# Latent attention: when the second half of the queries is made

## The chip, the cores and the metric

The kernel runs on one core of a Trainium2 chip. The metric is the device time of one launch in microseconds (us); the kernel before takes 2556.23 us (median of 3 runs, 2555.82 to 2557.56). All stages below run in that launch. Five engines work side by side and wait for each other through semaphores: TensorE (PE, matmuls into the PSUM banks), VectorE (DVE), ScalarE (ACT), GpSimd (POOL), and SyncE (SP), which starts the transfers of the weights. PEld is TensorE's loading of the stationary operand.

## The reference, cut to what matters

Two residual blocks work on 512 tokens of width 1024. The first has a mixer, a cross attention to a memory and a gated FFN; the second has two layers, of which the last holds the stage that is changed, `mla_mixer`, a latent attention of 8 heads:

```
lat = h @ w_in                                  # 768 query latent | 256 kv latent | 64 rotary key
q  = rmsnorm(cq, q_norm) @ w_q_up               # 8 heads x (128 plain + 64 rotary)
kv = rmsnorm(ckv, kv_norm) @ w_kv_up            # 8 heads x (128 key + 128 value)
q  = rope_tail(rmsnorm(q, q_head_norm)); k = rope_tail(rmsnorm(k, k_head_norm))
s  = q k^T * 192**-0.5, causal; p = softmax(s); o = p v
y  = o.reshape(S, 1024) @ w_out
```

All matrix products are kept near float32: each operand is split into a high part and a low part, and a product is made of three matmuls (high x high, low x high, high x low).

## The kernel before, in words

Everything is stored transposed, channels on the 128 partitions and the 512 tokens along the free axis. `linear` (L180 on) makes one output tile of 128 channels after another: a weight unit is fetched on SP's queue (`fetch`, L137), split by `cook` into `whi` on ACT (L146) and `wlo` on DVE (L148), and for each piece of the contraction `mm3` issues three matmuls (L176 to L178) into one PSUM bank. Then an eviction function reads the bank. There are three buffers each for the raw, the high and the low weights.

PSUM has eight banks, in groups with a tag each: `ps` 2, `sc` 2, `pt` 2, `po` 1, `mi` 1. SBUF tiles of 128 x 512 come from pools with tags too: `xs` 16, `cv` 9, `pr` 2, `m` 16, `q` 17, `t` 7. A tile of a tag can only be taken when one of that tag's buffers has been given back by its last reader.

The order of each engine's instructions is written by a planner while the program is built: it goes through the program text in a simulated time of its own and lets an engine take, of the instructions that are ready by its reckoning, the one that stands first in the text. On the chip every engine then runs its list strictly in that order.

The stage `mla` makes, in this order of the text: the kv and query latents; the raw keys of all heads (`kraw`); `values(0)`, the values of heads 0 to 3; then the queries, in twelve tiles of 128 channels (three for each pair of heads: two plain tiles and one that holds the rotary part of both). `ev_q` (L1083) evicts a query tile: it squares it (L320) and sums the squares with small matmuls into the bank `qsum` (L216), then splits a plain tile into `qn` (tag `xs`) or turns a rotary tile (`rope`, L459 to L464, on DVE and POOL) and packs it with `stack` (L472 on ACT, L474 on DVE) into `qp` (tag `cv`). After every sixth tile `inner_rstd` makes the scale of four heads, `fcol`: it reads `qsum` (L225), turns it on PE, and finds the inverse root in three Newton rounds of small DVE instructions (L235 to L243, ending at L271).

`key(h)` finishes a head's key: `spread` (two matmuls, L313 and L314) brings its scale across the partitions, ACT copies it to `bs` (L1104), POOL multiplies `kraw` (L1106) and the shared rotary key (`kp`, L1111) with it, and each is split into high (ACT, L193) and low (L195; on POOL for `kn`, on DVE for `kp`). `key(0)` is made after the sixth query tile, the other keys by `scores`.

`scores(h)` makes four blocks of 128 queries: three matmuls with the plain key, two with the rotary key (L1137 and L1138), one that adds the causal mask (L1140). `softmax_rows` takes the maximum (DVE, L445), multiplies it with the scale (L446), exponentiates (ACT, L448), inverts the sum (DVE, L449) and normalises (POOL, L450). `attend(h)` transposes the probabilities (L132, tag `pt`), splits them into `pth` and `ptl`, and multiplies them with the values into the bank `po`; the result is split into `os`. The order of the text is

```
scores(0); then for h = 0 to 7: scores(h + 1), attend(h), and values(1) after h == V_AT
```

with `V_AT` 1; `values(1)` are the values of heads 4 to 7. The product with `mla_w_out` and the last FFN follow.

Of the kernel before, what the change touches and what calls it, by code (L numbers as in the profile page):

```python
# [17 lines left out]
P = 128  # L18
# [43 lines left out]
class Kern:  # L62
# [939 lines left out]
                                scalar2=None, op0=ALU.mult)  # L1002


    V_AT = 1
    MLA_TAGS = ("pt", "mi")
    KEYS_EARLY = 1
    KEY_AT = 1
# [2 lines left out]
    def mla(self):  # L1011
        nc = self.nc
        a = self.a
        self.TR_TAG, self.BC_TAG = self.MLA_TAGS
        xs, R = self.pre("mixg1")
        rb = self.bcast(R)
        cq, ckv, st = [], [], {}
        sqs = {"q": [], "kv": []}
        cos, sin = self.cos2, self.sin2

        def ev_cq(nt, ps):
            sqs["q"] = self.gather(sqs["q"], self.square(ps), nt == 5)
            cq.append(self.split(ps, self.v("gql", nt), "q", name="cq"))

        def ev_ckv(nt, ps):
            sqs["kv"] = self.gather(sqs["kv"], self.square(ps), nt == 7)
            ckv.append(self.split(ps, self.v("gkvl", nt - 6), "q", name="ckv"))

        def ev_kpe(nt, ps):
            t = self.t("cv", name="kpe")  # L1030
            nc.vector.tensor_tensor(out=t, in0=ps, in1=rb, op=ALU.mult)
            st["sqpe"] = self.square(t)
            st["kpr"] = self.rope(t, "gkp", "gkps", cos, sin)

        w = a["mla_w_in"]
        tags = ("ps", "ps", "sc", "sc")
        ones = self.c("ones")
        self.linear(w, [6, 7], xs, ev_ckv, tags)
        self.linear(w, [8], xs, ev_kpe, ("sc",))
        Rkv = self.inner_rstd(self.sums([(ones, q) for q in sqs["kv"]]), 256, R)  # L1040
        bkv = self.bcast(Rkv, "pr")
        self.linear(w, range(6), xs, ev_cq, tags)
        Rq = self.inner_rstd(self.sums([(ones, q) for q in sqs["q"]]), 768, R)

        kraw = []
        pesum = self.y("pesum")[:, :8]
        nc.vector.tensor_copy(pesum.rearrange("p (j r) -> p j r", j=4), self.columns(
            self.sums([(self.c("blk64")[:, :32], st["sqpe"])]), 192, EPS, 2))
        ksum = self.ps("mi", "ksum")
        for u in range(2):  # L1050
            ws = self.tiles(self.load_unit(a["mla_w_k"][u]), 8)
            for hh in range(4):
                h = 4 * u + hh
                ps = self.ps(tags[hh])
                for k in range(2):
                    self.mm3(ps, ws[2 * hh + k], ckv[k], k == 0, k == 1)
                self.sums([(self.c("selh")[:, 32 * h:32 * h + 32], self.square(ps))], ps=ksum,
                          start=h == 0, stop=h == 7)
                t = self.t("m", name="kraw")
                nc.vector.scalar_tensor_tensor(out=t, in0=ps, scalar=self.v("gkn"), in1=bkv,  # L1060
                                               op0=ALU.mult, op1=ALU.mult)
                kraw.append(t)
        Rk = self.expand(self.key_rstd(ksum[:, :P], pesum, Rkv), 8, "pr")

        vs = [[None] * 4 for _ in range(2)]

        def values(c):
            hi, lo = self.load_unit(a["mla_w_v"][c])
            for tt in range(4):
                ts_ = slice(tt * P, (tt + 1) * P)  # L1070
                ps = self.ps(tags[tt])
                for k in range(2):
                    self.mm3(ps, (ckv[k][0][:, ts_], ckv[k][1][:, ts_]),
                             (hi[:, k * S:(k + 1) * S], lo[:, k * S:(k + 1) * S]), k == 0, k == 1)
                vs[c][tt] = self.split(ps, Rkv[:, tt:tt + 1],
                                       "m" if c == 0 or tt < 2 else "cv", name="v")

        values(0)

        qn, qp, fcol = [], [], []  # L1080
        qsum = self.ps("po", "qsum")

        def ev_q(nt, ps):  # L1083
            p, r = nt // 3, nt % 3
            sq = self.square(ps)
            i, o = p % 2, P * (p // 2)
            sel = self.c("selh")[:, 32 * (2 * i + r):32 * (2 * i + r) + 32] if r < 2 \
                else self.c("blk64")[:, 32 * i:32 * i + 32]
            self.sums([(sel, sq)], ps=qsum, o=o, start=nt % 6 == 0, stop=nt % 6 == 5)
            if r < 2:  # L1090
                qn.append(self.split(ps, self.v("gqn"), "xs", name="qn"))
            else:
                qr = self.rope(ps, "gqp", "gqps", cos, sin)
                for h in range(2):
                    qp.append(self.stack(qr, h, "cv"))
            if nt % 6 == 5:
                fcol.append(self.inner_rstd(qsum[:, o:o + P], 192, Rq, 4, post=192.0 ** -0.5))

        keys = {}

        def key(h):
            bp = self.spread(Rk, h, "mi")
            bs = self.t(name="bs")
            nc.scalar.copy(bs, bp)  # L1104
            kn = kraw[h]
            nc.gpsimd.tensor_tensor(out=kn, in0=kn, in1=bs, op=ALU.mult)  # L1106
            kns = self.t("t", F32R, name="knh"), self.t("t", F32R, name="knl")
            self.split_into(*kns, kn, on_pool=self.KN_POOL)
            kp = self.t(name="kp")
            eng = nc.gpsimd if self.KP_POOL else nc.vector  # L1110
            eng.tensor_tensor(out=kp, in0=st["kpr"], in1=bs if self.KP_POOL else bp, op=ALU.mult)  # L1111
            kps = self.big("kp", F32R)
            kps = kps[:, :S], kps[:, S:2 * S]
            self.split_into(*kps, kp, on_pool=self.KL_POOL)
            keys[h] = kns, kps

        for n in range(4):
            self.linear(a["mla_w_q"], range(3 * n, 3 * n + 3), cq, ev_q, tags[n:] + tags[:n])
            if n == self.KEY_AT:
                for h in range(self.KEYS_EARLY):  # L1120
                    key(h)
        prs, os = {}, []

        def scores(h):
            if h not in keys:
                key(h)
            kns, kps = keys.pop(h)
            q, qq = qn[h], qp[h]
            prs[h] = []
            for i in range(4):  # L1130
                w = P * (i + 1)
                W = max(256, w)
                js = slice(i * P, (i + 1) * P)
                sc = self.ps(("sc", "ps")[i % 2], "sc")
                self.mm3(sc[:, :W], (q[0][:, js], q[1][:, js]),
                         (kns[0][:, :W], kns[1][:, :W]), True, False)
                nc.tensor.matmul(sc[:, :W], qq[:, js], kps[0][:, :W], start=False, stop=False)  # L1137
                nc.tensor.matmul(sc[:, :W], qq[:, js], kps[1][:, :W], start=False,  # L1138
                                 stop=False)
                nc.tensor.matmul(sc[:, js], self.idb, self.mskb, start=False, stop=True)  # L1140
                prs[h].append(self.softmax_rows(sc, w, fcol[h // 4][:, 4 * i + h % 4:4 * i + h % 4 + 1], "q"))

        def attend(h):
            c, es = h // 4, slice((h % 4) * P, (h % 4 + 1) * P)
            po = self.ps("po", "po")
            for s in range(4):
                pt = self.ps("pt", "pt")
                for i in range(s, 4):
                    self.turn(pt[:, i * P:(i + 1) * P], prs[h][i][:, s * P:(s + 1) * P])
                z = s * P  # L1150
                hi, lo = self.t("q", F32R, name="pth"), self.t("q", F32R, name="ptl")
                o = min(z, 256)
                if o < z:
                    nc.gpsimd.memset(hi[:, o:z].bitcast(F32), 0.0)
                    nc.gpsimd.memset(lo[:, o:z].bitcast(F32), 0.0)
                self.split_into(hi[:, z:], lo[:, z:], pt[:, z:])
                vt = vs[c][s]
                self.mm3(po[:, o:], (vt[0][:, es], vt[1][:, es]), (hi[:, o:], lo[:, o:]),
                         s == 0, s == 3)
            del prs[h]  # L1160
            os.append(self.split(po, None, "xs", name="o"))

        scores(0)
        for h in range(8):
            if h < 7:
                scores(h + 1)
            attend(h)
            if h == self.V_AT:
                values(1)
        self.TR_TAG = self.BC_TAG = "mi"  # L1170
        self.linear(a["mla_w_out"], range(8), os, self.res_evac(1.0), tags)
# [235 lines left out]
```

## Time and profile before

| | |
|---|---|
| median of 3 runs | 2556.23 us |
| profiled execution | 2555.78 us |
| its span (first to last instruction) | 2554.0 us |
| mean granted clock of PE | 0.996 |
| PE busy | 2502.4 us, 98% of the span |
| DVE, ACT, POOL busy | 50%, 36%, 15% |
| transfers | 92 GB/s on average |
| PE's waits for transfers in the stage `mla` | none listed |

The times in the trace count from the start of the span. Matmuls overlap: a row of the timeline gives a matmul's start and the time until its result is there, and the pace is read from the starts. A wait in square brackets behind a row is the idle time of that engine just before it, with what ended it.

### The profile page before, as it was taken

The numbers are of one execution on the slowest core, as the hardware profiler recorded it, in microseconds if no ns is written. First come the engines' busy times: TensorE is split into PE (matmuls) and PEld (weight loads), VectorE is DVE, ScalarE is ACT, GpSimd is POOL, SyncE is SP. The second block draws the span as 40 slices with busy tenths as digits, with TensorE's granted clock in tenths as the row PEclk, the third lists the DMA queues.
The fourth block names the chain that finished last, engine by engine and source line by source line (L and its number), as shares of the span: only waits on it lengthen the run. The fifth ranks groups of instructions, "written<-read, shape, count | busy, mean of one in ns | idle before, by whom it ended". The sixth has DMA issues, their size and how long they took to land.

```text
span 2554.0 us, 29962 instructions
## 1 busy us (share of the span) xinstructions
PE 2502.4 (98%) x11996; PEld 2019.6 (79%) x11996; DVE 1272.0 (50%) x1819; ACT 916.6 (36%) x1324; POOL 372.0 (15%) x339
## 2 busy tenths in 40 slices
PE   8899999999999999999999999999999989999999
PEld 7657677788887888888888888888887767888887
DVE  5646453866623545435555533555334585555422
ACT  4444444544423332223333222333223455333311
POOL 0422112111100111102111100111001144111100
PEclk9999999999999999999999999999999999999999
DMA  5233212232232233333223333323332210322332
GB/s 190 67 109 114 67 59 74 75 99 99 88 98 87 91 99 99 93 92 121 89 93 100 99 97 97 97 93 99 91 99 91 75 58 25 99 95 95 97 106 78
DMA packets 71852, 236.04 MB, mean 92 GB/s; under 512 B 8544, under 2 KB 12256, under 8 KB 71712
## 3 DMA queue, kind: packets, MB, share of 16 engines
q1 hardware_dynamic: 70336, 231.60, 28.7%
q0 software_dynamic: 1232, 2.36, 0.3%
q8 instruction: 94, 1.54, 0.2%
q14 instruction: 46, 0.38, 0.0%
q10 hardware_dynamic: 144, 0.16, 0.0%
HBM read 227.84 MB, written 2.10 MB: 90 GB/s over the span
## 4 chain that ended last, share of the span: by engine, by line
PE 95%; DVE 3%; ACT 1%; issue 0%; DMA 0%; ACTq 0%
PE ps L177 28%; PE ps L176 28%; PE ps L178 28%; PE cps L587 1%; PE pt L132 1%; PE po L177 1%; PE sum L216 1%; PE po L176 1%; PE po L178 1%; PE wo L176 1%; PE wo L177 1%; PE wo L178 1%; PE bc L284 1%; PE sc L176 0%; DVE wlo L148 0%
## 5 line engine op out<-in xcount | busy, mean ns | idle before, releaser
L146 ACT CAST whi<-raw 128x1024 fp32r<-128x1024 f32 (+2 forms) x432 | 440.4, 1021 | 1217.5 <-PE ps L177 754.0
L148 DVE TENSOR_TENSOR wlo<-raw,whi 128x1024 fp32r<-128x1024 f32 (+2 forms) x428 | 590.7, 1382 | 517.3 <-ACT whi L146 512.1
L176 PE MATMUL ps<-xh,whi 128*128 128x512 f32 x2008 | 782.8, 391 | 7.7 <-ACT xh L197 6.9
L177 PE MATMUL ps<-xl,whi 128*128 128x512 f32 x2008 | 785.1, 391 | 3.2 <-DVE xl L378 2.5
L178 PE MATMUL ps<-xh,wlo 128*128 128x512 f32 x2008 | 781.6, 390 | 0.0
L176 PEld LDWEIGHTS ps<-xh,whi 128*128 128x128 f32 x2008 | 377.4, 188 | 88.6 <-ACT xh L197 6.9
L177 PEld LDWEIGHTS ps<-xl,whi 128*128 128x128 f32 x2008 | 377.5, 188 | 87.0 <-DVE xl L378 6.2
L178 PEld LDWEIGHTS ps<-xh,wlo 128*128 128x128 f32 x2008 | 377.4, 188 | 78.0 <-issue 0.6
L178 PE MATMUL ps<-ah,wlo 128*128 128x512 f32 x880 | 342.4, 389 | 0.0
L176 PE MATMUL ps<-ah,whi 128*128 128x512 f32 x880 | 342.4, 389 | 0.0
L177 PE MATMUL ps<-al,whi 128*128 128x512 f32 x880 | 342.4, 389 | 0.0
L884 DVE TENSOR_TENSOR g<-ps,bct 128x512 f32<-128x512 f32 x176 | 120.7, 691 | 392.0 <-PE ps L178 383.6
L889 POOL TENSOR_TENSOR g<-g 128x512 f32<-128x512 f32 x88 | 119.9, 1363 | 886.5 <-ACT whi L146 519.3
L176 PEld LDWEIGHTS ps<-ah,whi 128*128 128x128 f32 x880 | 165.2, 188 | 34.4
L178 PEld LDWEIGHTS ps<-ah,wlo 128*128 128x128 f32 x880 | 165.2, 188 | 34.3
L177 PEld LDWEIGHTS ps<-al,whi 128*128 128x128 f32 x880 | 165.2, 188 | 34.1
L327 POOL TENSOR_TENSOR sq<-sq 128x512 f32<-128x512 f32 x54 | 81.6, 1512 | 546.2 <-ACT sq L320 545.7
L193 ACT CAST ah<-g 128x512 fp32r<-128x512 f32 x88 | 54.8, 623 | 114.3 <-POOL g L889 114.3
L435 DVE SCALAR_TENSOR_TENSOR x<-ps,x 128x512 f32<-128x512 f32 x40 | 27.5, 691 | 84.5 <-PE ps L178 84.4
L448 ACT ACTIVATE p<-sc,nb,f 128x512 f32<-128x512 f32 (+3 forms) x80 | 53.4, 673 | 43.3 <-DVE nb L446 39.8
L195 DVE TENSOR_TENSOR al<-g,ah 128x512 fp32r<-128x512 f32 x88 | 63.1, 718 | 10.0 <-ACT ah L193 9.6
L450 POOL TENSOR_SCALAR p<-p,rl 128x512 f32<-128x512 f32 (+3 forms) x80 | 49.4, 623 | 123.0 <-DVE rl L449 120.0
(289 smaller groups left out, 2366.1 us busy)
## 6 DMA issues: line engine op xcount, KB each, us to landing
raw<-in_wgu SPq DMA_DIRECT2D x176, 512.0 KB, 3.7
raw<-in_wd SPq DMA_DIRECT2D x64, 512.0 KB, 3.5
raw<-in_w_up SPq DMA_DIRECT2D x44, 512.0 KB, 3.7
raw<-in_wd SPq DMA_DIRECT2D x32, 384.0 KB, 3.2
raw<-in_w_down SPq DMA_DIRECT2D x16, 512.0 KB, 3.6
raw<-in_w_in SPq DMA_DIRECT2D x14, 512.0 KB, 4.3
raw<-in_mla_w_in SPq DMA_DIRECT2D x9, 512.0 KB, 3.7
raw<-in_mla_w_q SPq DMA_DIRECT2D x12, 384.0 KB, 3.1
```

The lines of the kernel that those rows point to most:

```text
L146: self.nc.scalar.copy(hi[:, s], raw[:, s])
L148: eng.tensor_tensor(out=lo[:, s], in0=raw[:, s], in1=hi[:, s].bitcast(F32), op=ALU.subtract)
L176: mm(ps, w[0], x[0], start=start, stop=False)
L177: mm(ps, w[0], x[1], start=False, stop=False)
L178: self.mmi = mm(ps, w[1], x[0], start=False, stop=stop)
L193: nc.scalar.copy(hi, src)
L195: self.loi = eng.tensor_tensor(out=lo, in0=src, in1=hi.bitcast(F32), op=ALU.subtract)
L327: self.nc.gpsimd.tensor_tensor(out=sqs[0][:, :w], in0=sqs[0][:, :w], in1=sq[:, :w], op=ALU.add)
L448: nc.scalar.activation(p[:, :w], ps[:, :w], AF.Exp, bias=nb, scale=f, accum_out=l)
L450: nc.gpsimd.tensor_scalar(out=p[:, :w], in0=p[:, :w], scalar1=rl, scalar2=1.0, op0=ALU.mult, op1=ALU.mult)
L884: nc.vector.tensor_tensor(out=g, in0=ps, in1=rb, op=ALU.mult)
L889: nc.gpsimd.tensor_tensor(out=g, in0=g, in1=st["g"], op=ALU.mult)
```

## The change

`V_AT` becomes 2, and the text's order becomes

```
queries 0..5, key(0), scores(0), queries 6, 7, scores(1), query 8, attend(0),
queries 9, 10, 11, attend(1), scores(2); for h = 2 to 7: scores(h + 1), attend(h), values(1) after h == 2
```

Because six tiles of the query latent now stay in use until after heads 0 and 1, those two heads take other buffers (`early`): probabilities from `xs` in place of `q`, `pth` and `ptl` from `t`, the first output from `cv` and `q`, scores only from the banks `sc`, and the late query tiles only from the banks `ps`. The squares of the second half are summed in the bank `mi` in place of another part of the bank `po`; `key(1)` therefore spreads its scale in a bank of `ps`, the later keys in `mi` as before. No instruction is added or taken away. Cut to its core:

```diff
-    V_AT = 1
+    V_AT = 2
...
-        qsum = self.ps("po", "qsum")
...
+            if nt % 6 == 0:
+                qsum.append(self.ps(("po", "mi")[nt // 6], "qsum"))
...
-        def key(h):
-            bp = self.spread(Rk, h, "mi")
+        def key(h, early=False):
+            bp = self.spread(Rk, h, "ps" if early else "mi")
...
-        for n in range(4):
-            self.linear(a["mla_w_q"], range(3 * n, 3 * n + 3), cq, ev_q, tags[n:] + tags[:n])
-            if n == self.KEY_AT:
-                for h in range(self.KEYS_EARLY):
-                    key(h)
...
-                sc = self.ps(("sc", "ps")[i % 2], "sc")
+                sc = self.ps("sc" if early else ("sc", "ps")[i % 2], "sc")
...
-                prs[h].append(self.softmax_rows(sc, w, fcol[h // 4][:, 4 * i + h % 4:4 * i + h % 4 + 1], "q"))
+                prs[h].append(self.softmax_rows(sc, w, fcol[h // 4][:, 4 * i + h % 4:4 * i + h % 4 + 1],
+                    "xs" if early else "q"))
...
-                hi, lo = self.t("q", F32R, name="pth"), self.t("q", F32R, name="ptl")
+                hi, lo = (self.t("t" if early else "q", F32R, name=z) for z in ("pth", "ptl"))
...
-            os.append(self.split(po, None, "xs", name="o"))
-
-        scores(0)
-        for h in range(8):
+            os.append(self.split(po, None, tags[0], tags[1], name="o"))
+
+        def queries(nts, tags):
+            self.linear(a["mla_w_q"], nts, cq, ev_q, tags)
+
+        queries(range(6), tags)
+        key(0)
+        scores(0, True)
+        queries([6, 7], ("ps",))
+        scores(1, True)
+        queries([8], ("ps",))
+        attend(0, True, ("cv", "q"))
+        queries([9, 10, 11], ("ps",))
+        attend(1, True)
+        scores(2)
+        for h in range(2, 8):
```

## Rows read from the trace of the kernel before

**Rows 1.** The page's part 4: the chain that ended last, by engine.

```profile
PE 95%; DVE 3%; ACT 1%; issue 0%; DMA 0%; ACTq 0%
```

**Rows 2.** Stretches of 10 us: length, busy time (instructions), PE clock, DMA share, GB/s.

```profile
core 0: us, PE busy (x) PEld busy (x) DVE busy (x) ACT busy (x) POOL busy (x), PEclk, DMA share, GB/s
...
2070.00:2080.00 10.00, 4.97 (x23) 3.35 (x23) 9.64 (x19) 5.58 (x13) 8.64 (x10) 1.00 0.00 1
2080.00:2090.00 10.00, 8.57 (x38) 7.21 (x38) 7.30 (x21) 5.33 (x14) 6.48 (x8) 0.66 0.00 0
...
2110.00:2120.00 10.00, 10.00 (x66) 8.51 (x65) 7.98 (x28) 8.65 (x25) 9.10 (x14) 1.00 0.01 2
```

**Rows 3.** Waits of PE from 2060 to 2280: total us, times, longest us.

```profile
PE sc L1138 <- DVE kp L195: 5.5, 1, 5.5
PE po L176 <- DVE ol L195: 1.7, 2, 0.9
...
PE sc L176 <- ACT p L448: 0.8, 3, 0.3
...
PE bc L313 <- ACT bs L1104: 0.4, 1, 0.4
PE sc L176 <- ACT knh L193: 0.3, 1, 0.3
```

**Rows 4.** Timeline of PE: start us, us, engine, line, operation, shape, count [idle before].

```profile
2063.40 0.39 PE L178 MATMUL ps<-cqh,wlo 128*128 128x512 f32 x1
...
2066.42 0.48 PE L313 MATMUL bc<-Xh,s 128*128 128x512 f32 x1
...
2081.43 0.58 PE L1138 MATMUL sc<-kp,st 128*128 128x256 f32 x1 [5.48 <-DVE kp L195]
...
2084.91 0.41 PE L176 MATMUL sc<-knh,qnh 128*128 128x256 f32 x1
...
2086.19 0.52 PE L176 MATMUL sc<-knh,qnh 128*128 128x384 f32 x1
...
2087.56 0.39 PE L177 MATMUL sc<-knl,qnh 128*128 128x512 f32 x1
...
2099.18 0.28 PE L177 MATMUL sc<-knl,qnh 128*128 128x256 f32 x1
2099.30 0.28 PE L178 MATMUL sc<-knh,qnl 128*128 128x256 f32 x1
...
2113.69 0.60 PE L132 MATMUL pt<-con,p 128*128 128x128 f32 x4
```

**Rows 5.** Timeline of DVE (VectorE).

```profile
2055.12 0.17 DVE L271 SCALAR_TENSOR_TENSOR f<-y,f 128x16 f32<-128x16 f32 x1
...
2068.23 0.28 DVE L225 TENSOR_SCALAR q<-qsum 128x128 f32<-128x128 f32 x1
...
2077.45 0.17 DVE L242 TENSOR_TENSOR b<-b,y 128x16 f32<-128x16 f32 x1
...
2079.65 1.13 DVE L240 SCALAR_TENSOR_TENSOR b<-y,v 128x16 f32<-128x16 f32 x1
2080.70 0.68 DVE L195 TENSOR_TENSOR kp<-kp 128x512 fp32r<-128x512 f32 x1
```

**Rows 6.** Timeline of ACT (ScalarE).

```profile
2064.55 0.59 ACT L320 ACTIVATE sq<-ps 128x512 f32<-128x512 f32 x1
...
2067.83 1.28 ACT L448 ACT_TABLE_LOAD   x1
...
2073.93 0.62 ACT L193 CAST kp<-kp 128x512 fp32r<-128x512 f32 x1
...
2162.05 1.67 ACT L320 ACTIVATE sq<-x 128x512 f32<-128x512 f32 x3
...
2210.74 1.28 ACT L886 ACT_TABLE_LOAD   x1
```

**Rows 7.** Timeline of POOL (GpSimd).

```profile
2079.49 1.26 POOL L1111 TENSOR_TENSOR kp<-m,bs 128x512 f32<-128x512 f32 x1 [0.63 <-DVE st L474]
```

More of the change, by code (lines that the diff above doesn't have):

```diff
@@ L1078, in mla @@
         values(0)
-        qn, qp, fcol = [], [], []
-        qsum = self.ps("po", "qsum")
+        qn, qp, fcol, qsum = [], [], [], []
         def ev_q(nt, ps):
@@ L1085, in ev_q @@
             sq = self.square(ps)
-            i, o = p % 2, P * (p // 2)
+            i = p % 2
+            if nt % 6 == 0:
+                qsum.append(self.ps(("po", "mi")[nt // 6], "qsum"))
             sel = self.c("selh")[:, 32 * (2 * i + r):32 * (2 * i + r) + 32] if r < 2 \
                 else self.c("blk64")[:, 32 * i:32 * i + 32]
-            self.sums([(sel, sq)], ps=qsum, o=o, start=nt % 6 == 0, stop=nt % 6 == 5)
+            self.sums([(sel, sq)], ps=qsum[-1], start=nt % 6 == 0, stop=nt % 6 == 5)
             if r < 2:
@@ L1096, in ev_q @@
             if nt % 6 == 5:
-                fcol.append(self.inner_rstd(qsum[:, o:o + P], 192, Rq, 4, post=192.0 ** -0.5))
+                fcol.append(self.inner_rstd(qsum[-1][:, :P], 192, Rq, 4, post=192.0 ** -0.5))
         keys = {}
-        def key(h):
-            bp = self.spread(Rk, h, "mi")
+        def key(h, early=False):
+            bp = self.spread(Rk, h, "ps" if early else "mi")
             bs = self.t(name="bs")
@@ L1115, in key, with scores @@
             keys[h] = kns, kps
-        for n in range(4):
-            self.linear(a["mla_w_q"], range(3 * n, 3 * n + 3), cq, ev_q, tags[n:] + tags[:n])
-            if n == self.KEY_AT:
-                for h in range(self.KEYS_EARLY):
-                    key(h)
         prs, os = {}, []
-        def scores(h):
+        def scores(h, early=False):
             if h not in keys:
-                key(h)
+                key(h, early)
             kns, kps = keys.pop(h)
@@ L1140, in scores, with attend @@
                 nc.tensor.matmul(sc[:, js], self.idb, self.mskb, start=False, stop=True)
-                prs[h].append(self.softmax_rows(sc, w, fcol[h // 4][:, 4 * i + h % 4:4 * i + h % 4 + 1], "q"))
-        def attend(h):
+                prs[h].append(self.softmax_rows(sc, w, fcol[h // 4][:, 4 * i + h % 4:4 * i + h % 4 + 1],
+                    "xs" if early else "q"))
+        def attend(h, early=False, tags=("xs", "xs")):
             c, es = h // 4, slice((h % 4) * P, (h % 4 + 1) * P)
```

## The prediction

> **What bounds the kernel now.** I read the page's chain first: 95% of the span is TensorE (PE) [rows 1]. A change that adds and removes no instruction can only give back the time in which PE stands still or runs slowly, so I next cut the latent attention into stretches of 10 us. Two of them fall out of line: from 2070 to 2080 PE is busy for 4.97 us while VectorE (DVE) is busy for 9.64, and from 2080 to 2090 the granted clock is 0.66; a stretch of the heads further on has PE full at clock 1.00 [rows 2]. The waits of PE over the stage give the sizes: 5.5 us once, for the low half of a key's rotary part (`kp`, made on DVE), 1.5 us in five short waits about the first scores (0.8 + 0.4 + 0.3), and 1.7 us in two waits for `ol` deep in the heads [rows 3]. The queries end at 2063.40, the long wait stands before 2081.43 [rows 4]: it is the place where PE has used up the queries, and the first heads' softmax and keys are a chain of small steps on other engines. The change moves half of the queries behind that place.
>
> What does DVE do meanwhile? The high half of `kp` of head 1 was ready at 2073.93 + 0.62 = 2074.55 [rows 6], but its low half started on DVE only at 2080.70 [rows 5], 6.15 us later. In between DVE ran what the last query tile leaves behind: rotary products, stacks and the Newton steps that give the scales of heads 4 to 7 (`fcol[1]`). One such step on 16 columns took 0.17 us alone and 1.13 us where GpSimd (POOL) made a `kp` at the same time; it ended at 2080.78, POOL's instruction at 2080.75 [rows 5, 7].
>
> **The change, part by part.** The work is the same: twelve query tiles, eight heads, the same transfers in the same order on SP's queue (`mla_w_q`, `mla_w_v`, `mla_w_out`); only when a buffer comes free moves a little, and none of the waits in rows 3 is for a transfer. I price it by time of PE, against the profiled execution (2555.78 us, span 2554.0; 0.45 us under the median).
>
> *Removed, first:* the 5.5 us wait. *Second:* the slow stretch behind it. Six 256-column matmuls from 2084.91 to 2086.19 took 1.28 us, 0.213 each; at full pace one starts 0.12 us after another (2099.18, 2099.30), and from 2087.56 a 512-column one takes 0.39 us as everywhere else [rows 4]. The two paces fit the two levels of the clock, 1.2 and 2.4 GHz, with what does not scale between them. From 2081.43 to 2087.56 are 6.13 us; at 0.12 against 0.213 they would be 3.45, so 2.7 us go. *Third:* the five short waits, 1.5 us, which come from scores whose key or exp was not there; with queries 6 to 8 (PE always has one ready) beside them they are covered. Sum: -9.7 us, if PE never runs dry again.
>
> *Scales of the first half.* `scores(0)` now follows tile 5. Its matmuls need no scale, its exps do: `fcol[0]` was ready at 2055.12 + 0.17 [rows 5], and tiles 6 and 7 and the start of 8 cover PE until about then. Cost 0; without that cover it would be a wait of the old kind.
>
> *Interleaved stretch.* Heads 0 and 1 now share PE with tiles 6 to 11. Early scores have two banks (`sc`), the later tiles two (`ps`, which `key(1)` borrows too), where both groups shared four. The `xs` tiles (16) hold queries and the two early heads' probabilities, so tiles 9 and 10 can be evicted only as `attend(0)` gives back its own. No row shows this; from below it costs nothing (a full stretch like 2110 to 2120 [rows 2]), from above one more stall of the old kind, 5.5 + 2.7 = 8.2 us. I take 0.85 us, one wait of the size that the heads have [rows 3], since the heads are the nearest rows.
>
> *Behind the last tile.* The second `qsum` now lies in `mi`, where `key(2)` wants its `spread`. So `key(2)` cannot begin before the square, the sums and the L225 read of tile 11; on PE `scores(2)` stands behind its spread, and every later head behind that. Before, the last query matmul was through at 2063.40 + 0.24 = 2063.64, its square ended at 2064.55 + 0.59 = 2065.14 [rows 4, 6], and L225 takes 0.28 [rows 5]: at least 1.8 us. Then the chain of a key: from the spread at 2066.42 to the high half of `kp` at 2074.55, and 0.68 for the low half: 8.8 us [rows 4 to 6]. Together 10.6 us from the last tile until the next scores can be finished. What has PE for that time? `attend(1)`: 3 x (512 + 384 + 256 + 256) columns = 16.5 times 0.12, 2.0 us, and ten transposes at no more than 0.15 (four took 0.60), 1.5 us; two spreads, 2 x 2 x 512 columns, 0.96; the first four of the five products of `scores(2)`, 4 x 1408 columns, 2.64 [rows 4]. That is 7.1 us, so a wait of 3.5 us takes the place of the old one. Below it: 0, where `values(1)` or a late `attend(0)` fills it. Above: DVE again puts the low half 6.15 us behind its inputs, with 2.7 us of slow clock after it: 12.4 us. I take 3.5.
>
> Here a rule speaks against the change. Rows first: the step on DVE that ended with POOL's instruction, 1.13 against 0.17 us [rows 5, 7]. The Trainium skill, "SBUF — State Buffer", section "Who interferes with whom", says that VectorE and GpSimd share one port pair as an exclusive lock, so that one fully blocks the other. The trace agrees at this place. By that rule the Newton steps of `fcol[1]`, which still meet POOL's work for `key(2)`, stay as long as they were, and the term is nearer to its upper end.
>
> *`values(1)` one head later* (`V_AT` 2): the same 24 matmuls fill in behind head 2. Zero; at best it covers the two 0.85 us waits, -1.7.
>
> *Exp among squares:* the load of the exp table is there once (1.28 us at 2067.83); squares at 2162.05 run under it, and the next load is at 2210.74 [rows 6]. Nothing is reloaded, cost 0.
>
> Sum: -9.7 + 0.85 + 3.5 = -5.35 us; 2555.78 - 5.35 + 0.45 = 2551 us at the median.
>
> **Rivals.**
> - *Nothing takes the wait's place.* Both new terms are 0, and at best the 1.7 us go too: -9.7 to -11.4, 2545 to 2546.5 us. For it: PE full in a stretch of the heads where keys run ahead [rows 2]. Against it: `mi` is taken until tile 11 is summed.
> - *The stall only moves behind tile 11.* Rotary, stacks and Newton steps of tile 11 still come in one burst, `ptl` of `attend(1)` and the low half of `kp` queue behind them on DVE, and PE waits for those with nothing else. If half of the 6.15 us comes back, and the clock falls again: 3.5 + 3.1 + 2.7 = 9.3 in place of 3.5, sum +0.4: 2556.7, no change. For it: DVE 9.64 of 10 us [rows 2], and the lock above (Trainium skill, same page and section). Against it: POOL had a burst of probabilities there, which now comes earlier.
> - *Slower: the queries block behind the early heads.* Tiles 9 and 10 wait for `xs` tiles that `attend(0)` frees; with two `ps` banks the third tile behind them cannot start, PE's order is fixed, and `attend(0)` itself hangs on `fcol[0]`, exps and POOL's normalisation. A whole stall with slow clock is then added (8.2) while the end of the queries keeps its own (9.3): -9.7 + 8.2 + 9.3 = +7.8, 2564 us. It decides from the point where `attend(0)`'s first transposes come later than the end of tile 10, about 9 us of PE after tile 8. Against it: between `fcol[0]` and those transposes lies one softmax of four blocks, and tiles 8 and 9 (36 x 0.24 us of PE) stand beside it.
> - *The change does nothing,* because the planner orders PE as before: hardly possible, since `scores(0)` now stands ahead of tile 6; no chance of its own.
>
> **How the numbers follow.** Forecast 0.45 (own range 2547 to 2555), whole gain 0.22, stall moves 0.20, slower 0.13. A measurement of this kernel tells 0.2%, about 5.1 us, from no change. Half of the forecast's range lies beyond that: faster 0.23 + 0.22 = 0.45; within 0.22 + 0.19 = 0.41; slower 0.14. The range takes in the whole gain (2545) and the stall that moves with some spread (2560), and leaves out the slower rival: 2545 to 2560.
>
> **What would show it.** Right: no PE wait over 5 us, no stretch with a granted clock under 0.9, exps of head 0 between the query tiles, and after the last query matmul a wait of 2 to 5 us for `kp`, `knh` or `ptl`; the spread of head 2 right after L225 of tile 11. Wrong: a PE wait of 5 us or more behind tile 11 with the clock down after it (the stall moved), PE waiting at a query matmul for an eviction (`qnl`, `xs`) between heads 0 and 1 (slower), or no wait behind tile 11 at all, with `values(1)` in it (whole gain).

## The result, and the profile after

The changed kernel takes 2569.12 us (median of 6 runs, 2568.64 to 2571.18), the kernel before on the same chip 2556.03 us (6 runs): ratio 1.0053, 95% interval 1.0042 to 1.0063. It is 13 us slower, where 2551 us was forecast and 2545 to 2560 given as the range. The span of the profiled execution grew by 12.8 us, to 2566.8.

The chain of waits is PE's as before [rows 1], with one per cent more on DVE:

```profile
PE 94%; DVE 4%; ACT 1%; issue 1%; DMA 0%; POOL 0%; ACTq 0%
```

The stretches of 10 us that answer to [rows 2] (columns as there):

```profile
2040.00:2050.00 10.00, 7.55 (x57) 5.42 (x56) 8.65 (x25) 4.55 (x8) 3.72 (x3) 0.99 0.31 104
2050.00:2060.00 10.00, 5.92 (x20) 4.36 (x21) 3.45 (x11) 5.14 (x11) 2.13 (x4) 0.67 0.00 1
2060.00:2070.00 10.00, 10.00 (x42) 7.94 (x40) 3.62 (x7) 3.53 (x6) 3.82 (x3) 0.83 0.06 13
2070.00:2080.00 10.00, 10.00 (x57) 7.88 (x55) 6.83 (x16) 5.72 (x12) 2.85 (x6) 1.00 0.26 93
2080.00:2090.00 10.00, 7.10 (x49) 4.67 (x48) 5.32 (x10) 5.43 (x11) 0.88 (x3) 1.00 0.16 52
2090.00:2100.00 10.00, 7.28 (x27) 5.80 (x27) 9.12 (x26) 3.80 (x8) 2.98 (x4) 0.66 0.16 53
2100.00:2110.00 10.00, 8.81 (x39) 6.84 (x40) 4.60 (x15) 6.09 (x16) 8.44 (x9) 0.83 0.01 2
```

A rough gauge of PE's lost time is the length less busy time times clock. Before, the two stretches of [rows 2] that fall out of line lose 5.0 and 4.3 us, 9.4 in all, and the one from 2060 to 2070 loses 0.5. After, the seven stretches lose 2.5, 6.0, 1.7, 0, 2.9, 5.2 and 2.7, 21.0 in all: 11.2 more than the same seven before, most of the 13. The gauge is good to a few us only: claim_key2, a run below, loses by it as much from 2000 to 2130 as the kernel before (10.7 us each), and takes 4 us longer. One stall has become three: about 2047 to 2063, about 2080 to 2084, and from 2088 to 2105.

The waits of PE from 2000 to 2290 (total us, times, longest) no longer hold the 5.5 us for `kp` of [rows 3]. In its place stand:

```profile
PE sc L176 <- ACT p L448: 4.5, 2, 4.3
PE pt L132 <- POOL p L450: 2.2, 1, 2.2
PE tr L132 <- DVE q L225: 1.8, 1, 1.8
PE po L176 <- DVE ol L195: 1.7, 2, 0.9
PE qsum L216 <- ACT sq L320: 1.4, 1, 1.4
PE sc L176 <- ACT knh L193: 1.3, 1, 1.3
PE po L177 <- DVE ptl L195: 1.1, 1, 1.1
```

**The first stall.** PE's timeline (start, us, idle before in brackets): the last matmul of tile 7, the third block of `scores(0)`, a 512-column matmul at the low clock, the transposes of head 0, the first matmul of tile 8, and the first one at the usual pace again:

```profile
2044.99 0.39 PE L178 MATMUL ps<-cqh,wlo 128*128 128x512 f32 x1
...
2051.87 0.69 PE L176 MATMUL sc<-knh,qnh 128*128 128x384 f32 x1 [4.32 <-ACT p L448]
...
2054.30 0.63 PE L177 MATMUL sc<-knl,qnh 128*128 128x512 f32 x1
...
2059.32 0.44 PE L132 MATMUL pt<-con,p 128*128 128x128 f32 x2 [2.21 <-POOL p L450]
...
2060.41 0.75 PE L176 MATMUL ps<-cqh,whi 128*128 128x512 f32 x1
...
2063.51 0.39 PE L177 MATMUL ps<-cql,whi 128*128 128x512 f32 x1
```

Between tile 7 and tile 8 lie 15 us in which PE has only the rest of `scores(0)` and some transposes to do. After standing 4.3 us it goes on at the slow pace (a matmul of 512 columns takes 0.63 us at 2054.30, against 0.39 before and at 2063.51). Why tile 8 does not start is seen on ACT:

```profile
2042.29 0.60 ACT L320 ACTIVATE sq<-ps 128x512 f32<-128x512 f32 x1
...
2045.97 0.59 ACT L320 ACTIVATE sq<-ps 128x512 f32<-128x512 f32 x1
...
2051.27 0.46 ACT L448 ACTIVATE p<-sc,nb,f 128x128 f32<-128x128 f32 x1
...
2057.41 0.78 ACT L448 ACTIVATE p<-sc,nb,f 128x512 f32<-128x512 f32 x1 [1.75 <-DVE nb L446]
...
2058.18 1.26 ACT L197 ACTIVATE qnh<-ps,vec 128x512 fp32r<-128x512 f32 x2
```

Tiles 6 and 7 are squared at 2042.29 and 2045.97, but their `qnh` is written only at 2058.18, right behind the fourth exp of head 0. Until then both `ps` banks are full. ACT was idle for 3.41, 2.54 and 1.75 us before the exp table and the third and fourth exp, so it was not short of time.

**The second stall** has the same look. The last matmul of tile 9 starts at 2072.11, but its square comes 9 us later on ACT, behind the last two `pth` of `attend(0)`, which have the tag `t` as the square has, and the fourth exp of head 1; tile 11, which takes over tile 9's bank, starts at 2083.55:

```profile
2079.95 0.54 ACT L193 CAST pth<-pt 128x256 fp32r<-128x256 f32 x2 [0.94 <-PE pt L132]
...
2081.15 0.61 ACT L320 ACTIVATE sq<-ps 128x512 f32<-128x512 f32 x1
```

No run tests this one by itself.

**The third stall**, behind tile 11: its last matmul, the sums, the turn of `qsum`, the spread of head 2 and its first scores on PE; and on ACT the last `pth` of `attend(1)` with `bs` of head 2 right behind it:

```profile
2087.55 0.39 PE L178 MATMUL ps<-cqh,wlo 128*128 128x512 f32 x1
2089.34 0.43 PE L216 MATMUL qsum<-sq,con 128*32 128x128 f32 x8 [1.41 <-ACT sq L320]
2091.58 0.48 PE L132 MATMUL tr<-con,q 128*128 128x128 f32 x1 [1.81 <-DVE q L225]
...
2092.56 0.78 PE L313 MATMUL bc<-Xh,s 128*128 128x512 f32 x1
...
2100.80 1.36 PE L176 MATMUL sc<-knh,qnh 128*128 128x256 f32 x4 [1.32 <-ACT knh L193]
```

```profile
2097.36 0.27 ACT L193 CAST pth<-pt 128x128 fp32r<-128x128 f32 x1 [0.48 <-PE pt L132]
2097.52 0.59 ACT L1105 COPY bs<-bc 128x512 f32<-128x512 f32 x1
```

### The profile page after: what moved, and what is told of

Its sections match the earlier page's. It is cut to its first block, busy times and chain, and to the rows that moved or that the text cites. A ratio compares the mean times of both kernels' runs of the same rounds, so it can differ in the third digit from the quotient of the medians.

```text
span 2566.8 us, 29971 instructions
## 1 busy us (share of the span) xinstructions
PE 2508.8 (98%) x11996; PEld 2023.8 (79%) x11996; DVE 1269.3 (49%) x1819; ACT 918.4 (36%) x1324; POOL 369.4 (14%) x339
## 4 chain that ended last, share of the span: by engine, by line
PE 94%; DVE 4%; ACT 1%; issue 1%; DMA 0%; POOL 0%; ACTq 0%
PE ps L177 28%; PE ps L176 28%; PE ps L178 28%; PE cps L587 1%; PE pt L132 1%; PE po L177 1%; PE sum L216 1%; PE po L176 1%; PE wo L176 1%; PE po L178 1%; PE wo L177 1%; PE wo L178 1%; PE bc L284 1%; DVE wlo L148 0%; PE sc L176 0%
```

## The experiments

Six theories were set against each other. **A:** the planner hands out the buffers of a tag in the order in which the text first writes them, free or not, so `qnh` of tiles 6 and 7 (tag `xs`) stands behind the probabilities of head 0, and `bs` of head 2 (tag `t`) behind the `pth` of `attend(1)`. **B:** the bank `mi` holds `key(2)` behind tile 11. **C:** two score banks make the exps of an early head wait for each other. **D:** DVE's Newton rounds, slow beside GpSimd, come ahead of what PE waits for. **E:** `key(2)` is started too late, whatever holds it. **F:** each gap that is closed opens the next. Times are medians; the ratio is to the kernel before on the same chip.

### A: who holds tiles 6 and 7 (claim_xs)

```diff
-                qn.append(self.split(ps, self.v("gqn"), "xs", name="qn"))
+                qt = ahead.pop(0) if ahead else (self.t("xs", F32R, name="qnh"),
+                                                 self.t("xs", F32R, name="qnl"))
...
+        for _ in range(2):            # ahead of scores(0)
+            ahead.append((self.t("xs", F32R, name="qnh"), self.t("xs", F32R, name="qnl")))
+            for z in ahead[-1]:
+                nc.gpsimd.memset(z[:, :P].bitcast(F32), 0.0)
```

> Kernel: the changed one, with four small writes on GpSimd (128 columns each) ahead of scores(0) that take the four xs buffers of query tiles 6 and 7 before the probabilities of head 0 take theirs. Theory A (a tag's buffers go out in the text's order, so the evictions of tiles 6 and 7 wait for the softmax of head 0, both ps banks stay full and tile 8 cannot start): the gap between the end of tile 7 (2045) and the start of tile 8 (2060.4) closes to under 4 us, qnh of tile 6 comes ahead of the exps of head 0, the two waits of PE there (4.3 for the exp, 2.2 for the normalisation) and the slow clock of 2050 to 2070 go; 6 to 10 us less than the changed kernel, 2559 to 2563. Theory C (two score banks make the exps of a head wait for each other): the wait of 4.3 us for the exp stays at blocks 2 and 3 of head 0, time within 3 us of the changed kernel, 2566 to 2570. Theory B (the bank mi holds key(2) behind tile 11) says nothing on this gap and expects 2566 to 2570 too. Under none of them should the gap behind tile 11 shrink.

2564.58 us, 1.0032 (1.0020 to 1.0045): faster than the changed kernel (1.0053) by 5 us, a little less than expected. On ACT both `qnh` now follow their squares at once, and the first exp comes 8 us after the second of them:

```profile
2042.05 0.60 ACT L320 ACTIVATE sq<-ps 128x512 f32<-128x512 f32 x1
2042.67 0.69 ACT L197 ACTIVATE qnh<-ps,vec 128x512 fp32r<-128x512 f32 x1
...
2045.74 0.59 ACT L320 ACTIVATE sq<-ps 128x512 f32<-128x512 f32 x1
2046.23 0.68 ACT L197 ACTIVATE qnh<-ps,vec 128x512 fp32r<-128x512 f32 x1
...
2054.38 0.46 ACT L448 ACTIVATE p<-sc,nb,f 128x128 f32<-128x128 f32 x1
```

On PE tile 8 starts at 2047.70 in place of 2060.41, and the waits of 4.3 and 2.2 us are gone:

```profile
2047.70 0.50 PE L176 MATMUL ps<-cqh,whi 128*128 128x512 f32 x1
```

So four `xs` buffers were free at 2042; only the order kept them. This part of theory A is shown. But part of the gain is lost again: PE's waits now hold

```profile
PE po L177 <- DVE ptl L195: 2.3, 2, 1.4
PE ps L176 <- DVE qnl L198: 2.3, 1, 2.3
```

The second is tile 11, which waits for the bank of a tile whose `qnh` stands behind the fourth exp of head 1: a hold-up of the same look three tiles on. Whether the order made it or buffers not yet given back, no run shows.

### A, B and E: what holds key(2) (key2_ahead, key2_bank, key2_far, claim_key2)

```diff
         queries([9, 10, 11], ("ps",))
+        key(2, True)                  # key2_ahead
         attend(1, True)
+        key(2, True)                  # key2_bank (this line alone)
         scores(2)
```

> Kernel: the changed one, with key(2) in the text before attend(1), and its spread in a ps bank. Theory A: bs of key(2) is copied before the pth of attend(1), right after the sums of tile 11, so knh and kp of head 2 come about 5 us earlier; the scores of head 2 start without the slow stretch before them; 3 to 6 us less than the changed kernel, 2563 to 2566. Theory B alone: the spread no longer waits for the read of qsum (2.0 us), so about 2 us less, 2567. Rival D (the chain of small DVE steps of tile 11 and the Newton rounds, which take 1.13 us against POOL's instructions, set the scale of head 2's queries and keys): no gain, 2567 to 2570.

> Kernel: the changed one, with the spread of key(2) in a ps bank in place of mi, at the same place of the text. Theory A: bs of key(2) still follows the last pth of attend(1), because both have the tag t; no change, 2568 to 2570. Theory B (the bank decides): the spread and bs come 2 us or more earlier and scores(2) with them, 2 to 6 us less, 2563 to 2567.

key2_ahead: 2571.25 us, 1.0057 (1.0045 to 1.0070); key2_bank: 2569.90 us, 1.0055 (1.0041 to 1.0068). Neither differs from the changed kernel. Theory B falls: in key2_bank the spread of head 2 starts 0.2 us after tile 11's last matmul in place of 5.0, but `bs` is copied 9.3 us after it in place of 10.0, still behind the last `pth`. One thing may hide a small gain in both traces: behind the same two waits as in the changed kernel (0.2 and 1.1 us), the first eight matmuls of tile 11 ran at the slow pace here, so tile 11 ended 9.4 us after tile 10 in place of 7.8. Theory A for this stall made the right prediction of the order and the wrong one of the time: in key2_ahead `bs` is copied at 2093.41, ahead of the `pth`, and `knh` at 2095.43, yet the low half of `kp` still comes late, 2.4 us after the high half was there. On ACT and then DVE:

```profile
2098.82 0.62 ACT L193 CAST kp<-kp 128x512 fp32r<-128x512 f32 x1 [2.76 <-POOL kp L1112]
```

```profile
2097.62 1.20 DVE L235 TENSOR_SCALAR i<-v 128x16 int32<-128x16 int32 x1
2098.86 1.21 DVE L237 TENSOR_SCALAR y<-i 128x16 int32<-128x16 int32 x1
...
2101.87 0.68 DVE L195 TENSOR_TENSOR kp<-kp 128x512 fp32r<-128x512 f32 x1
```

The Newton rounds of the second scale stand ahead of it again, as in the kernel before [rows 5], and two of their steps take 1.2 us beside POOL's `kp` and its rotary product `m` (L464). Next, `key(2)` three tiles earlier, without and with the claim of claim_xs:

```diff
         scores(1, True)
+        key(2, True)                  # key2_far; claim_key2 has the claim as well
         queries([8], ("ps",))
```

> Kernel: the changed one with key(2) right after scores(1) in the text, no claim of buffers. Theory E with A: the gap at tile 8 (2047 to 2060) stays as in the changed kernel, the one behind tile 11 shrinks by 5 to 7 us: 2562 to 2565. Rival F: 2566 to 2571; it could be longer than the changed kernel, since key(2) takes two buffers of tag t that the early pth and ptl want.

> Kernel: claim_xs with key(2) made, in the text, right after scores(1), so ahead of query tiles 8 to 11 and of both early attends. Theory E (behind tile 11 PE idles because the whole chain of key(2), from its spread to the low half of kp, starts only then, and DVE puts that low half behind the Newton rounds; it does not matter which bank or which tag holds it back): knh and kp of head 2 are ready when the last query tile ends, the scores of head 2 stand beside tiles 10 and 11, the lost time of PE from 2080 to 2105 falls from about 12 us to under 6; 5 to 8 us less than claim_xs, 2556 to 2560. Rival F (each gap that is closed opens the next, since softmax and split of heads 0 and 1 on ACT, DVE and POOL take their time whatever PE has beside them): the gap moves to the transposes of head 0 or 1, and the time stays within 3 us of claim_xs, 2562 to 2567.

key2_far: 2570.92 us, 1.0052 (1.0040 to 1.0065), no gain. claim_key2: 2561.44 us, 1.0017 (1.0008 to 1.0026), 4 us below claim_xs by the ratios (the intervals overlap a little), a little short of the 5 to 8 expected. So the early key seems to be worth something only where tile 8 is not held up: in key2_far PE's waits for exps rose to 6.1 us, from 4.5. That is theory E with much of F.

### C: the score banks (banks_alone, claim_key2_banks)

```diff
-                sc = self.ps("sc" if early else ("sc", "ps")[i % 2], "sc")
+                sc = self.ps(("sc", "pt" if h == 0 else "sc")[i % 2] if early else ("sc", "ps")[i % 2], "sc")
```

> Kernel: the changed one with the four score blocks of head 0 in four banks (sc and pt), and nothing else. Theory A: the order of tag xs still holds tiles 6 and 7 in their banks until the exps of head 0 are through; the wait of 4.3 us for the exp goes, but PE then waits at tile 8 in its place; 2567 to 2570. Theory C: the wait goes with its slow clock, 5 to 8 us less than the changed kernel, 2562 to 2565.

> Kernel: claim_key2, with the four score blocks of head 0 in four banks (sc and pt) in place of the two of sc. Theory C (what is left of the gap at tile 8 is the third block of scores(0), which waits for the exp of the first to free its bank, 2.0 us with slow clock after it, and the exps wait for the scale of the first heads, ready at 2054.9): the wait goes, tile 8 runs before 2057, 2 to 4 us less than claim_key2, 2557 to 2559.5. Theory D (DVE's small steps, which take 1.1 to 1.2 us beside POOL's instructions in place of 0.17, make the scale late, and PE's fixed order waits for it in some place whatever banks there are): within 1.5 us of claim_key2, 2560 to 2563.

banks_alone: 2568.73 us, 1.0049 (1.0036 to 1.0063). As theory A said, the wait of 4.3 us for the exp went, and PE stood instead 4.0 us for the normalised probabilities and 2.8 us at a query tile for `qnl`. claim_key2_banks: 2559.83 us, 1.0013 (1.0005 to 1.0022), 1 us below claim_key2 by the ratios; the intervals overlap, so C is at most a small part.

### Other orders of the text (one_head_early, tile8_first)

```diff
         queries(range(6), tags)
         key(0)
+        queries([6, 7], ("ps",))      # tile8_first: [6, 7, 8], and four banks for head 0
         scores(0, True)
-        queries([6, 7], ("ps",))
-        scores(1, True)
-        queries([8], ("ps",))
+        key(1, True)
+        queries([8, 9], ("ps",))      # tile8_first: [9]
         attend(0, True, ("cv", "q"))
-        queries([9, 10, 11], ("ps",))
-        attend(1, True)
+        key(2, True)
+        queries([10, 11], ("ps",))
+        scores(1)
         scores(2)
+        attend(1)
```

> Kernel: the changed one with another order of the text: queries 0 to 5, key(0), queries 6 and 7, scores(0), key(1), queries 8 and 9, attend(0), key(2), queries 10 and 11, scores(1), scores(2), attend(1), then as before. Only head 0 takes the early buffers (xs, t, banks sc); head 1 has the buffers and the four score banks that the later heads have. Theory A with E: nothing that the query tiles need stands behind a softmax in the order of a tag, except tile 10 behind attend(0), and at the end of the queries two heads' scores are ready to run; lost time of PE from 2040 to 2105 of 6 to 10 us (23 in the changed kernel, 14 in the one before), 2548 to 2554. Rival F: the time that the softmax of head 0 and head 1 takes comes back as a wait between tile 9 and 10 and again before attend(1); 2556 to 2564.

> Kernel: one_head_early with tile 8 ahead of scores(0) in the text, and the four score blocks of head 0 in four banks. Theories A, C and E together: the scale of the first heads (about 2055) is there when scores(0) is through, tile 9 stands behind it, two heads' keys run beside tiles 9 to 11, and no gap over 2 us is left before tile 11; what remains is behind tile 11, where the exps of heads 1 and 2 and DVE's Newton rounds meet. 5 to 9 us less than one_head_early: 2553 to 2557. Theory D: 2558 to 2562.

2562.49 us, 1.0023 (1.0014 to 1.0032), and 2562.58 us, 1.0020 (1.0011 to 1.0029). Both miss what A, C and E together promised (2548 to 2554, 2553 to 2557). In one_head_early PE waits 6.1 us in six pieces for exps; in tile8_first 3.3 us for the normalisation and 2.0 us for squares of query tiles. Rival F has the better of it here.

### D in the changed kernels (kp_on_dve, claim_key2_banks_late, tile8_first_late)

```diff
-    KN_POOL, KP_POOL, KL_POOL = True, True, False
+    KN_POOL, KP_POOL, KL_POOL = True, False, False     # kp_on_dve, on claim_key2
...
+            nc.vector.tensor_scalar(out=eps, in0=after, scalar1=0.0, scalar2=EPS, op0=ALU.mult,
+                                    op1=ALU.add)       # the two others: after = last maximum of head 2
-        nc.vector.tensor_scalar(out=v, in0=v, scalar1=EPS, scalar2=None, op0=ALU.add)
+        nc.vector.tensor_scalar(out=v, in0=v, scalar1=eps, scalar2=None, op0=ALU.add)
```

> Kernel: claim_key2 with the product that makes kp on DVE (from the spread in PSUM) in place of GpSimd, for all heads. Theory D: one of POOL's three 1.3 us instructions of a key no longer meets the Newton rounds, so fewer of DVE's 16-column steps take over 1 us and the scale of heads 0 to 3 is ready 1 to 2 us earlier; DVE has 8 x 0.7 us more to do; 0 to 4 us less than claim_key2, 2557 to 2561. If DVE is short of time in the heads instead, 2 to 6 us more, 2563 to 2568.

> Kernel: claim_key2_banks, with the Newton rounds of the second scale made to wait for the last maximum of head 2 in the same way. Theory D: the waits for exps and kp between 2086 and 2104 shrink by 2 to 4 us: 2555.5 to 2558. If the interleaving itself costs the rest: within 1.5 us of claim_key2_banks, 2558.5 to 2561.5.

> Kernel: tile8_first, with the Newton rounds of the second scale made to wait for the last maximum of head 2. Theory D: behind tile 11 the scores of heads 1 and 2 no longer wait for exps held up by these rounds; 4 to 7 us less than tile8_first: 2555.5 to 2558.5. If the interleaving itself costs the rest: 2561 to 2564.

kp_on_dve: 2564.66 us, 1.0027 (1.0017 to 1.0038), no faster than claim_key2 and by the medians 3 us slower: PE now waits 3.7 us for banks that DVE's `kp` reads. tile8_first_late: 2563.85 us, 1.0026 (1.0016 to 1.0036), no gain. claim_key2_banks_late: 2565.76 us, 1.0034 (1.0021 to 1.0048), 5 us slower than without the delay. Let go after head 2, the rounds run from 2093.85 to 2103.90 on DVE, six of their steps at 1.14 to 1.27 us beside POOL's work for the keys, and the low half of the next head's `kp`, whose high half was there at 2098.65, comes behind them; on DVE, and on PE:

```profile
2096.81 1.22 DVE L240 SCALAR_TENSOR_TENSOR b<-y,v 128x16 f32<-128x16 f32 x1
...
2103.82 0.69 DVE L195 TENSOR_TENSOR kp<-kp 128x512 fp32r<-128x512 f32 x1
```

```profile
2104.56 0.58 PE L1148 MATMUL sc<-kp,st 128*128 128x256 f32 x1 [4.95 <-DVE kp L195]
```

That is the stall of the kernel before [rows 3 to 5], made again at another head: the rounds cost what stands behind them, some 5 us here. In these two runs the turn of `qsum` on PE moves in the text together with the rounds, and in claim_key2_banks_late it is this turn (on PE at 2093.34), not the epsilon (2089.74), that comes last before them. As an account of what is left in the changed kernels theory D finds no support, since these runs took nothing away from it.

### The kernel before, and its own wait (before_vat2, before_key1, before_late_scale, before_scale_head3, before_scale_pool, before_scale_head3_vat2)

```diff
-    V_AT = 1
+    V_AT = 2                          # before_vat2
...
-            if n == self.KEY_AT:
-                for h in range(self.KEYS_EARLY):
-                    key(h)
+            if n in (1, 2):           # before_key1
+                key(n - 1)
```

> Kernel: the one before with values(1) after head 2 in place of head 1, which is the one part of the change that stands by itself. As predicted, 0 (2555 to 2558); if values(1) filled time at head 1 that is now open, 2 to 5 us more.

> Kernel: the one before, with key(1) made after the ninth query tile in place of within scores(1); nothing else. If the 5.5 us wait before was a key that was started too late (its kp behind the last query tile's work on DVE), it goes without any reordering of the queries, with the slow clock behind it: 5 to 9 us less than the kernel before, 2547 to 2551. If PE there lacks work whichever key is first (softmax of head 0 is the next to be late), the wait turns into one for ptl or pth of head 0 and the time stays within 3 us, 2553 to 2559.

before_vat2: 2555.84 us, 0.9997 (0.9988 to 1.0006): `V_AT` costs nothing, as predicted, so the 13 us belong to the rest of the change, the moved queries with their buffers and banks. before_key1: 2560.12 us, 1.0014 (1.0005 to 1.0023), slower: the wait for `kp` is gone, but 4.9 us of waits for exps in five pieces and 1.5 us for `tr` stand in its place. So the early key is not enough there either.

The delay of the Newton rounds, here in the kernel before, behind head 1 (before_late_scale) or head 3 (before_scale_head3), and with the rounds on GpSimd:

```diff
                 scores(h + 1)
+            if h == 2:                # before_late_scale: h == 0, with the turn of qsum here too
+                fcol[1] = fcol[1](self.mx)      # the rounds, with eps from the last maximum
...
-            nc.vector.scalar_tensor_tensor(out=b, in0=y, scalar=-0.5, in1=v, ...)
+                eng.tensor_tensor(out=b, in0=y, in1=v, op=ALU.mult)     # before_scale_pool: eng is nc.gpsimd
```

> Kernel: the one before, with the Newton rounds of the second scale (fcol of heads 4 to 7) made to wait for the last maximum of head 1, by an epsilon that is computed from that maximum; one DVE instruction more, the text otherwise as before. Theory D: the low half of kp of head 1 follows its high half (2074.55) within about 1.5 us in place of 6.15, since only the two stacks of tile 11 stand before it; the wait of 5.5 us shrinks to 0 to 1.5 and the slow clock behind it goes; 5 to 8 us less than the kernel before, 2549 to 2552. Rival F: the next thing is late (softmax of head 0, or its transposes) and PE waits there; 2554 to 2558.

> Kernel: the one before, with the Newton rounds of the second scale made to wait for the last maximum of head 3 (one DVE instruction more). Theory D: both the wait for kp (5.5) and the one for ptl of head 0 (2.9 in before_late_scale) go, and the heads 3 and 4 have the cover for some 10 short steps of DVE: lost time of PE from 2060 to 2100 of 5 to 7 us in place of 13; 2549 to 2553. Rival F (something else is late in the first heads whatever DVE does, or the rounds make a new wait at head 3 or 4): 2554 to 2559.

> Kernel: the one before, with the three Newton rounds of the second scale on GpSimd (twelve small instructions there in place of nine on DVE); only the two integer steps and the last product stay on DVE. Theory D: as before_scale_head3, 2549 to 2553, if twelve small steps on POOL take under 5 us and the keys on POOL come no later for it. Rival: POOL's own queue (knl, kp, normalisation of heads 0 and 1) is late by those steps, and PE waits for knl or p: 2555 to 2561.

before_late_scale: 2557.59 us, 1.0004 (0.9996 to 1.0013), rival F's answer. On DVE the low half of `kp` comes at 2076.82, with only the two stacks ahead of it, and its 5.5 us wait is gone; the rounds now stand in front of the first `ptl` of head 0:

```profile
2076.82 0.85 DVE L195 TENSOR_TENSOR kp<-kp 128x512 fp32r<-128x512 f32 x1
...
2086.63 1.20 DVE L240 SCALAR_TENSOR_TENSOR b<-y,v 128x16 f32<-128x16 f32 x1
2087.76 0.68 DVE L195 TENSOR_TENSOR ptl<-pt,pth 128x512 fp32r<-128x512 f32 x1
```

and PE waits for that (total us, times, longest):

```profile
PE po L177 <- DVE ptl L195: 2.9, 1, 2.9
```

before_scale_head3: 2554.46 us, 0.9992 (0.9983 to 1.0000). before_scale_pool: 2554.90 us, 0.9992 (0.9983 to 1.0001). The stretches of before_scale_head3 (columns as in [rows 2]):

```profile
2070.00:2080.00 10.00, 8.23 (x41) 5.53 (x42) 7.39 (x20) 6.71 (x15) 9.17 (x9) 1.00 0.09 35
2080.00:2090.00 10.00, 8.69 (x50) 6.66 (x49) 6.95 (x25) 7.76 (x22) 9.27 (x11) 1.00 0.01 2
2090.00:2100.00 10.00, 10.00 (x57) 8.52 (x55) 8.12 (x15) 9.41 (x20) 7.79 (x12) 1.00 0.00 1
2100.00:2110.00 10.00, 8.54 (x54) 6.60 (x52) 9.78 (x28) 5.79 (x15) 8.20 (x11) 1.00 0.16 53
2110.00:2120.00 10.00, 8.82 (x52) 6.94 (x52) 8.71 (x32) 6.68 (x20) 5.06 (x7) 1.00 0.01 2
```

No wait for `kp` is left and the clock stays at 1.00: by the gauge above, 2070 to 2090 lose 3.1 us in place of 9.4. But 2100 to 2120 (the second half full before, [rows 2]) lose 2.6: heads 3 and 4, where the rounds now run and DVE is busy for 9.78 of 10 us from 2100. The last run put `values(1)` beside them (`V_AT = 2`):

> Kernel: before_scale_head3 with values(1) after head 2 in place of head 1, so beside the late Newton rounds. If the gain was given back because values(1) was used up too early: the waits between 2100 and 2120 shrink by 2 to 3 us, 2551 to 2553. If DVE and GpSimd pace the heads in any case: within 1.5 us of before_scale_head3, 2553 to 2556.

before_scale_head3_vat2: 2554.07 us, 0.9990 (0.9981 to 0.9999). It is the fastest of all, 2.8 us below the kernel before; the step from 0.9992 is within the error. The wait that the change was meant to remove can be removed with the queries where they were, but in these three runs that is worth 2 to 3 us, which the intervals hardly tell from no change, and not 10.

## Why the prediction was wrong

- *The removal* (-9.7) took place in its first two parts: no wait for `kp` of 5.5 us is left, and the slow stretch behind it has gone with it. The third part, the 1.5 us of short waits for exps, `bs` and `knh`, did not: 4.5, 0.6 and 1.3 us are lost for these now. The price stands against 9.4 by the gauge. That it would be kept is what failed; before_late_scale and before_key1 show that other chains are late at the same place, 2.9 and 4.9 us, and before_scale_head3 that the same removal without moved queries is worth 2 to 3 us. One reading was off: between 2074.55 and 2080.70 DVE ran Newton steps and two stacks, the rotary products had been made before.
- *Interleaved stretch*, taken at 0.85 with 8.2 as the upper end, is the step that failed. From 2040 to 2090 PE loses 13.1 us by the gauge (11.8 up to 2088.2, where tile 11's matmuls end). The prediction counted the `xs` buffers (there are enough for tiles 6 and 7) and looked for a hold-up at tiles 9 and 10; it did not ask in which order the buffers go out. The text puts head 0's four probabilities ahead of tile 6. claim_xs shows this and its price, 5 us; that more than one stall of the old kind could stand in the stretch, the upper end had not allowed.
- *Scales of the first half*, cost 0: the scale was ready earlier than expected (2049.64 in place of 2055.29), and still the cover failed, because the start of tile 8 that was to give it lay behind the exps that the scale serves. PE stood for 4.3 us at the third block of `scores(0)`, the wait of the old kind that the prediction named for this case.
- *Behind the last tile*, taken at 3.5 with 12.4 as the upper end: 2090 to 2110 lose 7.9 us (9.3 from 2088.2). The size lies within the bounds, the mechanism was wrong: another bank than `mi` brings `bs` no more than 0.7 us forward (key2_bank), and PE waits for `sq`, `q` and `knh`, with slow clock, not for `kp`. With tile 8 freed, an earlier key brings some 4 us (claim_key2 against claim_xs). The rounds do stand ahead of the low half of `kp` once `key(2)` comes earlier (key2_ahead), where their steps L235 and L237 take 1.20 and 1.21 us beside POOL's work; in the changed kernel they take 0.17 at 2046.04 and 2046.99. The Trainium skill, "SBUF — State Buffer", section "Who interferes with whom", says that on the port pair which VectorE and GpSimd share one of the two blocks the other fully, and that a VectorE instruction with one SBUF input is free of this unless it runs in a two-port mode. The trace agrees in the time; these two steps have one input, and no row shows their mode. The effect did not decide the sign.
- *`values(1)`*, 0: right (before_vat2). *Exp among squares*, 0: right; the exp table is loaded once, at 2049.97, and squares follow the exps without a load at 2081.15. (Its 1.28 us now lie inside the first stall.)
- *The rivals.* The slower rival (0.13) named the right kind of stall, two full `ps` banks and a fixed order on PE, but at tiles 9 and 10, for buffers not yet given back, and at +7.8. It came three tiles earlier, for buffers that were free, and at +13 in all. Tile 9 was held up too, for its square (the second stall). The point from which it was to decide, `attend(0)`'s transposes against the end of tile 10, was therefore the wrong test.
- *The sum:* forecast -9.7 + 0.85 + 3.5; by the gauge -9.8 + 13.1 + 7.9 = +11.2, measured +13.1.

What stays open: claim_key2_banks, with the order, the key and the banks mended, is still 1.0013. Its trace lists, among others, 3.6 us of PE's waits in four pieces for squares of query tiles, 1.8 us for an exp and 1.6 us in three for `ptl`, but no run shows which of them the rest is; the tests of D on it failed. That the interleaving gives several short chains fewer free buffers and banks each is a reading of the waits, not shown. Nor is it shown why heads 3 and 4 give back part of what before_scale_head3 gains.

## What to carry to other kernels

When a step is moved in a text that a planner turns into orders, go through each tag that it shares and write down who is handed a buffer before whom: enough buffers in number is not enough. A stall that several chains reach at nearly the same time is worth what the second of them leaves, so price the next late chain before the first is taken away. Small work that is wanted only much later (here the rounds of a scale for head 4) can be put behind a dependence in place of moving big work around it, but only to a place where nothing urgent queues behind it: behind head 3 it gained 2 to 3 us, behind head 1 nothing, and behind head 2 in claim_key2_banks it cost 5.

## What the runs showed of the hardware

The granted clock fell behind the long stands of PE: behind that of 4.3 us before 2051.87 it was 0.67 and 0.83 in the two stretches from 2050 on, where the matmuls behind it ran at half pace. In before_scale_head3, whose single waits from 2060 to 2130 are 1.3 us at most, it stayed at 1.00 in every stretch shown, although PE stood idle for about 3 of the 20 us from 2070 on. Several short waits cost their own length there, and the one long one cost more than that. But short waits are not safe by themselves. In the changed kernel waits of 1.41 and 1.81 us stand before a stretch at 0.66 (2090 to 2100), and in before_key1 none of PE's waits is over 1.7 us and the clock from 2070 to 2080 is 0.66. Behind waits of 0.2 and 1.1 us tile 11 began at the full pace in the changed kernel (clock 1.00 from 2080 to 2090) and at the slow pace in key2_ahead and key2_bank (0.83). What decides between them these runs do not show.
